# Last chunk of the MLP's second product: one seven-product run over all 1,024 output columns, in place of seven products for one half and a plain product for the other

## The chip, the cores and the metric

The kernel runs on one core of a Trainium2 chip. The metric is the device time of one execution in microseconds (us); lower is better. The engines are TensorE (PE in the profile; its weight loads are PEld), VectorE (DVE), ScalarE (ACT), GpSimd (POOL) and SyncE (SP, which here only issues DMAs). SBUF is the core's on-chip memory, PSUM the accumulators that TensorE writes; a PSUM bank holds 128 x 512 f32.

## What is computed

The reference is one decoder layer on 512 tokens of width 1,024. The change touches only its end:

```python
D_MODEL, SEQ, D_FF = 1024, 512, 4096
...
        x = x + merged @ w_out[l]
        h = rms_norm(x, norm_mlp[l])
        x = x + jnp.square(jax.nn.relu(h @ w_ff1[l])) @ w_ff2[l]
    return rms_norm(x, norm_final)
```

Everything is float32. TensorE multiplies in its faster fp32r form, so each operand is split into a high and a low part, and a product is three matmuls: high by high, high by low, low by high.

## The kernel before

**Chunks.** The hidden width of 4,096 is worked in four chunks of 1,024 (c = 0 to 3). In each chunk the first product makes 1,024 hidden columns for all 512 tokens, and the second product multiplies them by the chunk's 1,024 rows of `w_ff2` and adds the result into the residual `XX` (`x` in the profile), which stays in SBUF as four token tiles of 128 x 1,024.

**Seven products.** Most products are done in Strassen-Winograd form: both operands are cut into 2 x 2 blocks, and seven block products (named A11, S1, S3, A12, A22, S2, S4 after the weight block that each uses) take the place of eight. S1 to S4 are sums of the blocks A11 to A22 of the weight. The products share work: U is the A11 product (less the S2 product in the form before), and it is added into several quadrants of the result by the `fold` step.

**The second product, chunks 0 to 2** (class `Wide`, L1563): each of the seven products covers 512 output columns in two weight tiles (group g = 0, 1, each 128 x 1,024 floats = two k blocks of 512 columns), 12 matmuls of 512 columns for each tile.

**The second product, chunk 3** (`LAST`, L1872 to L1947): the left 512 output columns go by seven products of 256-column matmuls (class `Out`, L1517, 24 matmuls of 256 columns each, matmul line L1534). The right 512 columns are a plain product: four weight tiles of 256 rows (`f2310` to `f2313`), kept in the tiles R_64 and R_65 (`keep`), and for each of the four token tiles 24 matmuls of 512 columns (`last_half`, matmul line L505). The plain product of the token tiles 0 and 1 stands behind A11, S1 and A12; those of the token tiles 2 and 3 stand at the very end, the last one cut in two blocks of 256 columns. So the tokens of tiles 0 to 2 are normalized and sent out while TensorE still works for tile 3.

**A weight tile's way** (`group_steps`, L337): a DMA issued by SyncE brings it into one of five `raw` buffers; ScalarE copies the high part into one of three slots (wh, wh again, w3h; L357); VectorE subtracts to make the low part (wl, w3l; L360); TensorE reads both; the slot comes free when TensorE has done with it. The first use of a tile therefore waits for ScalarE, the second matmul for VectorE. Sums of weight blocks are made in two ways: in DRAM by DMAs (a copy, then an accumulating DMA issued by GpSimd, `make_sum` and `add_sum`), or in SBUF by VectorE from two raw buffers that lie there anyway (`SUMS`, L369, and L346 for the fourth). In chunk 3 before, all four sums of the left half come from DRAM.

**The order of the work** is written out by the program: `LAST_TURN` gives the turn of the products, `add_turn` the order of the loads, `ahead` (L479) starts the preparation of tiles up to three ahead, and side generators (`step_side`) interleave the steps on the results. Each engine then works its queue strictly in order.

**The hidden part** (class `Hidden`, L1764): its blocks get the same Winograd sums and high and low splits on VectorE and ScalarE (L1780, L1783, L1790, L1791, L1803 to L1817). In chunk 3 it also splits block 12 (into xT2), which only the plain product needs.

**The end**: for each token tile two square sums on ScalarE (L1502), one root and one reciprocal, two `scalar_tensor_tensor` on VectorE (L1514), and a DMA of 512 KB out. The last token tile is done in pieces on three engines (L1932 to L1947), with a 128 x 704 product on GpSimd (L1936).

Of the kernel before, what the change touches and what calls it, by code (L numbers as in the profile page):

```python
# [62 lines left out]
def trunk(ctx: ExitStack, tc: tile.TileContext, A, out):  # L63
# [124 lines left out]
    LAST_TURN = ("A11", "S1", "A12"), ("S3", "A22", "S2", "S4")  # L188

    def quarters(layer, c, g):  # L190

        if layer == 2 and c < LAST:
# [3 lines left out]
        w, r, o = ((w_f1, 0, 1024 * c + 512 * g), (w_f2, 1024 * c, 512 * g))[layer - 1]  # L196
        return {f"{i + 1}{j + 1}": w[r + 512 * j:r + 512 * j + 512, o + 256 * i:o + 256 * i + 256].rearrange(
            "(k p) c -> p k c", p=128) for i in range(2) for j in range(2)}

    def add_group(layer, c, g):  # L200
# [3 lines left out]
        final = layer == 2 and c == LAST  # L204
        for o in ("S1", "S3", "S2", "S4")[:4 if final else 4 - layer]:
# [7 lines left out]
        if final:  # L213
            jobs.append((of["S2"], of["S3"], q["22"]))
            jobs.append((of["S4"], of["S2"], q["12"]))
# [3 lines left out]
    SUMS = {"S2": "S4", "A12": "S4"}, {"S3": "S2", "A22": "S2", "S2": "S4"}  # L219

    def add_turn(layer, c, of, turn):
        for g, o in turn:
            key = f"{o}{layer}{c}{g}"
            to = SUMS[layer - 1].get(o) if "S4" not in of[g] else None
            if to:
                SUM_OF[key] = f"{to}{layer}{c}{g}"
            if layer == 2 and "S4" not in of[g] and o == "S4":
# [8 lines left out]
    for c in range(4):  # L236
# [98 lines left out]
    def rows_of(key):  # L335

        return 2 if key[-3] == "2" and int(key[-2]) < LAST else 4  # L337

    def group_steps(i):
# [15 lines left out]
        h, l = slot_of(i)  # L355
# [11 lines left out]
        else:  # L367
            yield
            DVE.tensor_tensor(t, t, held[to], op=ALU.add)  # L369
# [3 lines left out]
    kept = {}  # L373
# [1191 lines left out]
    class Wide(Out):  # L1565
# [40 lines left out]
        def fold(self):  # L1606
            for i, j in ((0, 1), (1, 0), (1, 1)):
                for f in range(2):
# [4 lines left out]
                    yield  # L1613

# [149 lines left out]
    class Hidden:  # L1764
# [4 lines left out]
        def __init__(self, last):  # L1769
            self.last = last  # L1770
# [4 lines left out]
        def of(self, b):  # L1775
            return XB["T2"] if b == "12" else YB[b]
# [22 lines left out]
        def sums(self, f):  # L1799
# [8 lines left out]
            if self.last:  # L1808
                yield from self.split("12", f, f12)
# [12 lines left out]
        def plain_of(self, k, t):  # L1822
            x = self.of(f"{k // 4 + 1}{t // 2 + 1}")
            return [y[:, k % 4, 128 * (t % 2):128 * (t % 2) + 128] for y in x]

    def in_turn(groups, turn):

        seen = {}
        for o in turn:
            n = seen.get(o, 0)  # L1830
            seen[o] = n + 1
            groups[n].pe(o)

    mode["pool"] = False
    for c in range(4):
        Y = Hidden(c == LAST)
# [35 lines left out]
    def last_half(w, t, cols=slice(0, 512), rows=range(4)):  # L1872

        prods = []
        for i in rows:
            for k in range(2):
                prods += split_products(*Y.plain_of(2 * i + k, t), w[i][0][:, k, cols], w[i][1][:, k, cols])
        return prods

    def folded():  # L1880
        yield from head.fold()
        for t in range(NT):
            square_sum(t, 0)
            yield
            if t < 2:
                finish(t)
                yield

    head = Out(LAST, 0, Y)
    keep([f"f2{LAST}1{i}" for i in range(4)], OT)  # L1890
    in_turn([head], LAST_TURN[0])
    w = []
    ps = [bank() for _ in range(2)]
    for i in range(4):
        w.append(use(f"f2{LAST}1{i}"))
        for t in range(2):
            mms(ps[t], last_half(w, t, rows=[i]), first=i == 0, last=i == 3)
            ahead()
            step_side()
    for t in range(2):  # L1900
        add_x(t, 1, ps[t])
        square_sum(t, 1)
    in_turn([head], LAST_TURN[1])
    gB = GBf[:, 0:D]
    nc.sync.dma_start(gB, bcast(A["norm_final"], D))
    while head.done != set(head.X):
        step_side()
    side.append(folded())
    END = 768
    xe = [x[:, 0, :] for x in XB["T3"]]  # L1910
    ACT.activation(xe[0], X1[3][:, END:], AF.Copy)
    DVE.tensor_tensor(xe[1], X1[3][:, END:], xe[0].bitcast(F32), op=ALU.subtract)
    for t in (2, 3):
        for c, n in (((0, 512),) if t == 2 else ((0, 256), (256, 256))):
            ps = bank()[:, 0:n]
            prods = last_half(w, t, slice(c, c + n))
# [49 lines left out]
```

## Time and profile before

| | |
|---|---|
| median of 3 runs | 787.26 us (786.37 to 789.39) |
| the profiled execution's own time | 786.53 us |
| its span, first to last instruction | 784.8 us |
| mean granted TensorE clock | 0.998 |
| busy: PE, DVE, ACT, POOL | 98%, 84%, 64%, 22% of the span |

The span is what the profile's clock covers; 1.73 us of the execution lie around it. In the rows of the timeline the columns are the start in us from the span's beginning, the duration in us, the engine, the line, the operation, out<-in by the program's names (without buffer numbers), the shape and the count; in square brackets stands the idle time before it and what ended it. A row with x2 merges two instructions. The last chunk's second product begins 735.3 us into the span and the last instruction of the chain that ends it is at 780 us; it takes 6% of the span.

### The profile page before, as it was taken

What the parts mean: (1) busy time and instruction counts of PE and PEld (TensorE: products, weight loads), DVE (VectorE), ACT (ScalarE), POOL (GpSimd) and SP (SyncE); (2) the same over time, 40 slices, a digit from 0 to 9 for tenths busy, and PEclk for the clock granted to TensorE, in tenths of its full rate; (3) what the DMA queues carried; (4) which work ended last, traced back from release to release, by engine and by line L of the source; (5) the groups of instructions that cost most, each with busy time, mean ns of one, the idle gap of its engine ahead of it and who ended that gap; (6) DMA issues with size and microseconds to landing.
All of it is one profiled execution on the core that took longest, in us unless ns stands there. A gap on an engine that the chain in (4) does not pass through costs nothing. (4 is left out here: it accounts for less than half of the span.)

```text
span 784.8 us, 13451 instructions
## 1 busy us (share of the span) xinstructions
PE 766.2 (98%) x4795; PEld 681.7 (87%) x4795; DVE 659.1 (84%) x1274; ACT 505.0 (64%) x977; POOL 175.2 (22%) x257
## 2 busy tenths in 40 slices
PE   7999999999999999999999999999999999999996
PEld 6889889888878888888889899879997999799996
DVE  6999868557989988998689689997899789998974
ACT  6668545337978888899545576944783478347833
POOL 4000000016847766553000120111110111010001
PEclk9999999999999999999999999999999999999999
DMA  9463732474565731011667998979998999897522
GB/s 306 129 165 98 198 95 91 116 209 122 77 162 112 165 66 41 28 55 50 170 212 210 286 239 241 299 172 312 306 268 221 309 282 286 213 273 219 189 78 108
DMA packets 118013, 140.80 MB, mean 179 GB/s; under 512 B 5477, under 2 KB 94729, under 8 KB 117770
## 3 DMA queue, kind: packets, MB, share of 16 engines
q1 hardware_dynamic: 98026, 116.64, 46.0%
q0 software_dynamic: 19632, 22.55, 19.2%
q8 instruction: 38, 0.62, 0.3%
q10 hardware_dynamic: 288, 0.75, 0.3%
q14 instruction: 29, 0.24, 0.1%
HBM read 135.20 MB, written 47.19 MB: 232 GB/s over the span
## 5 line engine op out<-in xcount | busy, mean ns | idle before, releaser
L505 PE MATMUL psF<-R,wh 128*128 128x512 f32 x448 | 144.3, 399 | 0.7 <-ACT scratch L876 0.7
L357 ACT ACTIVATE wh<-raw 128x1024 fp32r<-128x1024 f32 x70 | 73.8, 1058 | 70.0 <-PE psB L575 27.4
L319 POOL DMA_DIRECT2D S<-w_ff x40 | 45.1, 1128 | 307.3 <-DMA S<-w_ff 202.0
L360 DVE TENSOR_TENSOR wl<-raw,wh 128x1024 fp32r<-128x1024 f32 x70 | 85.3, 1221 | 18.5 <-ACT wh L357 18.3
L1323 POOL TENSOR_SCALAR P<-P,sm,GT 128x128 f32<-128x128 f32 (+3 forms) x128 | 85.2, 683 | 69.8 <-DVE sm L1320 44.4
L505 PEld LDWEIGHTS psF<-R,wh 128*128 128x128 f32 x448 | 80.5, 188 | 14.5 <-ACT scratch L876 0.9
L505 PE MATMUL psF<-R,wl 128*128 128x512 f32 x224 | 88.4, 394 | 1.3 <-DVE wl L464 1.3
L462 ACT ACTIVATE wh<-raw 128x512 fp32r<-128x512 f32 (+1 forms) x84 | 50.0, 620 | 55.9 <-PE psF L505 30.0
L1310 ACT ACTIVATE P<-P,sm 128x128 f32<-128x128 f32 (+3 forms) x128 | 71.2, 559 | 8.8 <-DVE sm L1300 6.0
L464 DVE TENSOR_TENSOR wl<-raw,wh 128x512 fp32r<-128x512 f32 (+1 forms) x82 | 56.6, 705 | 21.3 <-ACT wh L462 20.9
L1300 DVE CUSTOM_DVE_ANT_0 P<-psS,cst 128x128 f32<-128x128 f32 (+3 forms) x128 | 59.6, 483 | 4.6 <-PE psT L1340 2.5
L575 PE MATMUL psB<-R,wh 128*128 128x256 f32 x336 | 60.0, 279 | 0.0
L1356 DVE TENSOR_TENSOR PT<-psT,PT 128x512 fp32r<-128x512 f32 (+2 forms) x96 | 56.3, 592 | 3.5 <-ACT PT L1351 3.0
L357 ACT ACTIVATE w3h<-raw 128x1024 fp32r<-128x1024 f32 x35 | 37.0, 1058 | 31.2 <-PE psB L575 13.3
L1351 ACT ACTIVATE PT<-psT 128x512 fp32r<-128x512 f32 (+2 forms) x96 | 49.3, 522 | 12.0 <-PE psT L1340 10.9
L575 PEld LDWEIGHTS psB<-R,wh 128*128 128x128 f32 x336 | 51.4, 188 | 0.2
L505 PEld LDWEIGHTS psF<-R,wl 128*128 128x128 f32 x224 | 42.0, 188 | 10.4 <-DVE wl L464 1.7
L1340 PE MATMUL psT<-ident,P 128*128 128x128 f32 x320 | 50.1, 272 | 0.2 <-DVE PT L1356 0.2
L1374 PE MATMUL psO<-PT,VV 128*128 128x256 f32 x320 | 48.5, 286 | 0.0
L360 DVE TENSOR_TENSOR w3l<-raw,w3h 128x1024 fp32r<-128x1024 f32 x35 | 42.8, 1222 | 6.0 <-ACT w3h L357 5.9
L1340 PEld LDWEIGHTS psT<-ident,P 128*128 128x128 f32 x320 | 39.7, 140 | 8.9 <-issue 1.3
L575 PE MATMUL psB<-R,wl 128*128 128x256 f32 x168 | 46.9, 279 | 0.0
(487 smaller groups left out, 2210.1 us busy)
## 6 DMA issues: line engine op xcount, KB each, us to landing
raw<-w_ff SPq DMA_DIRECT2D x55, 512.0 KB, 6.8
S<-w_ff POOLq DMA_DIRECT2D x40, 512.0 KB, 8.4
raw<-S SPq DMA_DIRECT2D x40, 512.0 KB, 5.3
raw<-w_in SPq DMA_DIRECT2D x32, 512.0 KB, 4.0
S<-w_ff SPq DMA_DIRECT2D x30, 512.0 KB, 7.3
S<-S SPq DMA_DIRECT2D x10, 512.0 KB, 6.4
raw<-w_proj_nsa SPq DMA_DIRECT2D x8, 512.0 KB, 4.0
x<-x SPq DMA_DIRECT2D x7, 512.0 KB, 6.2
```

Of the source, the lines that this page charges most:

```text
L357: ACT.activation(h, t, AF.Copy)
L360: DVE.tensor_tensor(l, t, h.bitcast(F32), op=ALU.subtract)
L462: ACT.activation(h[:, sl], t[:, sl], AF.Copy)
L464: eng.tensor_tensor(l[:, sl], t[:, sl], h[:, sl].bitcast(F32), op=ALU.subtract)
L505: PE.matmul(ps, a, b, start=first and j == 0, stop=last and j == n - 1, skip_group_check=True)
L575: PE.matmul(out, w[u][:, k, 128 * f:128 * f + 128], moving[v][:, k, :], **kw)
L1300: DVE.tensor_tensor_reduce(out=P[:, o:o + n].rearrange("p (a c) -> p a c", c=128), in0=s, in1=m, scale=1.0, scalar=3e38, op0=ALU.add, op1= ...
L1310: last_exp[:] = [ACT.activation(c, c, AF.Exp, bias=sm[:, 0, e:e + 1], scale=-1.0, accum_out=sm[:, 1, e:e + 1])]
L1323: r = POOL.tensor_scalar(P[:, o:o + n], P[:, o:o + n], sm[:, 2, e:e + 1], GT[:, qb, c + e:c + e + 1], op0=ALU.mult, op1=ALU.mult)
L1340: PE.transpose(pt[:, 128 * j:128 * j + 128], P[:, 128 * j:128 * j + 128], ident)
L1351: ACT.activation(dH, src, AF.Copy)
L1356: return DVE.tensor_tensor(dL, src, dH.bitcast(F32), op=ALU.subtract)
```

## The change

For chunk 3 the new class `Whole` (a form of `Wide`) runs the seven products over all 1,024 columns, like the other chunks, in the turn A11, S1, S3, A22, S2, A12, S4. It differs from `Wide` in four ways.

1. No product accumulates on another one's PSUM bank, and U is the A11 product alone. VectorE adds each product straight from PSUM into every quadrant that needs it (`QUADS`, `take`: two for S1, two for S3, three for S2, one each for A22, A12, S4; two 128 x 512 additions for each quadrant).
2. GpSimd adds U into all four quadrants (`fold`: eight additions of 128 x 512). The additions for the last two quadrants stand behind the first two weight sums in GpSimd's queue (`pooled`).
3. The weight sums S2 = S3 + A22 and S4 = S2 + A12 are made in SBUF by GpSimd (four additions of 128 x 1,024), not in DRAM. S4's tiles go to the kept tiles R_64 and R_65.
4. S4, the last, works only on the right half of the tokens (token tiles 2 and 3, left 512 columns): 12 matmuls of 512 columns for tile 2, then two blocks of 12 matmuls of 256 columns for tile 3. Token tiles 0 and 1 are complete after A12.

The plain product, its four weight tiles, the split of block 12 and the function `folded` go. The end of the last token tile keeps its form with other column numbers.

```diff
-    LAST_TURN = ("A11", "S1", "A12"), ("S3", "A22", "S2", "S4")
+    LAST_TURN = ("A11", "S1", "S3", "A22", "S2", "A12", "S4")
...
-    SUMS = {"S2": "S4", "A12": "S4"}, {"S3": "S2", "A22": "S2", "S2": "S4"}
+    SUMS = [{"S2": "S4", "A12": "S4"}, {"S3": "S2", "A22": "S2", "S2": "S4"}]
+    SUMS.append(SUMS[0] | SUMS[1])
...
         else:
             yield
-            DVE.tensor_tensor(t, t, held[to], op=ALU.add)
+            last = key[-3:-1] == f"2{LAST}"
+            r = (POOL if last else DVE).tensor_tensor(t, t, held[to], op=ALU.add)
+            if last:
+                pooled.append(r)
             give_back(held[to])
             held[to] = t
...
+    class Whole(Wide):
+        AFTER = {}
+        QUADS = {"S1": ((1, 1), (0, 1)), "S3": ((1, 1), (1, 0)), "A22": ((1, 0),),
+                 "S2": ((1, 0), (1, 1), (0, 1)), "A12": ((0, 0),), "S4": ((0, 1),)}
+
+        def take(self, o, ps):
+            yield
+            if o == "A11":
+                for f in range(2):
+                    ACT.activation(self.U[:, f, :], ps[f], AF.Copy)
+                side.append(self.fold())
+            else:
+                for q in self.QUADS[o]:
+                    for f in range(2):
+                        self.add(DVE, q, f, ps[f], o == "S2")
+                        self.added(o, q, f)
+                    yield
+            self.done.add(o)
+
+        def add(self, eng, q, f, y, minus=False):
+            i, j = q
+            x = XX[:, 2 * j + f, 512 * i:512 * i + 512]
+            eng.tensor_tensor(x, x, y, op=ALU.add if bool(i) == minus else ALU.subtract)
...
+        def fold(self):
+            for q in ((0, 1), (1, 1), (1, 0), (0, 0)):
+                while q[1] == 0 and len(pooled) < 2:
+                    yield
+                for f in range(2):
+                    with behind(pooled[1]) if q[1] == 0 else nullcontext():
+                        self.add(POOL, q, f, self.U[:, f, :])
+                    yield
+                    yield
...
+    class Last(Whole):
+        def added(self, o, q, f):
+            t = 2 * q[1] + f
+            if o == "S2" and q[0] == 1:
+                square_sum(t, 1, 0)
+            elif o == "A12":
+                square_sum(t, 0, 1)
+                finish(t)
+
+    whole = Last(LAST, Y)
+    keep([f"S42{LAST}{g}" for g in range(2)], OT)
+    for o in LAST_TURN[:-1]:
+        whole.pe(o)
...
+    ps = bank()
+    for _ in pieces(ps, whole.ends(0)(slice(0, 512))):
+        step_side()
...
+    whole.add(DVE, (0, 1), 0, ps)
+    square_sum(2, 0, 1)
...
+    finish(2)
+    t, o, prods = 3, out_of(3), whole.ends(1)
+    for c in (END, 0):
+        ps = bank()[:, 0:256]
+        for _ in pieces(ps, ([(identR, x) for x in xe] if c == 0 else []) + prods(slice(c, c + 256))):
             step_side()
...
+        if c:
+            POOL.tensor_tensor(o[:, 320:D], X1[t][:, 320:D], gB[:, 320:D], op=ALU.mult)
```

How the queues stand is shown in two places. The first is GpSimd's queue from the last accumulating DMA to the end of the program. S_ tiles are sums in DRAM, raw_ the loaded weight tiles, x the residual, MA holds U and the output tiles, and GB the norm's weights. Before:

```order
L319 DMA S_131_108<-w_ff 512x1x256 [waits DMAHW6_49,DMASW0_49]
L319 DMA S_230_111<-w_ff 512x1x256 [waits DMAHW2_49,DMASW1_49]
L319 DMA S_230_112<-w_ff 512x1x256 [waits DMAHW7_49,DMASW2_49]
L1936 TENSOR_TENSOR MA<-x_4759,GB 128x704 [waits DMAHW5_49,DMAHW7_49,DVE_49,Activation_49]
L1943 TENSOR_SCALAR MA<-MA,sq 128x256 [waits DVE_49,Pool_49]
```

And in the changed kernel:

```order
L310 DMA S_231_112<-w_ff 256x1x512 [waits DMAHW6_49,DMASW2_49]
L1634 TENSOR_TENSOR x_4759<-x_4759,MA 128x512 [waits DVE_49,Activation_49]
L1634 TENSOR_TENSOR x_4759<-x_4759,MA 128x512 [waits DVE_49]
L1634 TENSOR_TENSOR x_4759<-x_4759,MA 128x512 [waits DMAHW5_49,Activation_49]
L1634 TENSOR_TENSOR x_4759<-x_4759,MA 128x512 [waits DVE_49]
L361 TENSOR_TENSOR raw_4766<-raw_4766,raw_5131 128x1024 [waits DMAHW2_49,DMAHW0_49,DVE_49]
L361 TENSOR_TENSOR raw_5170<-raw_5170,raw_5110 128x1024 [waits DMAHW3_49,DMAHW7_49,DMAHW1_49,DVE_49]
L1634 TENSOR_TENSOR x_4759<-x_4759,MA 128x512 x4
L361 TENSOR_TENSOR raw_5149<-raw_5149,raw_4766 128x1024 [waits DMAHW4_49,DVE_49,Pool_49]
L361 TENSOR_TENSOR raw_5131<-raw_5131,raw_5170 128x1024 [waits DMAHW6_49,DVE_49,Pool_49]
L1947 TENSOR_TENSOR MA<-x_4759,GB 128x704 [waits DMAHW5_49,DVE_49]
```

Twelve additions have come between the last DMA and the 128 x 704 product: eight of U and four of weight tiles, each with both inputs in SBUF.

The second place is VectorE's queue in the middle of the last chunk's second product. wl, w3l and R_65 are low parts of weight tiles, psB is a product in PSUM, and "waits Pool" is a wait for GpSimd. Before:

```order
L360 TENSOR_TENSOR wl_4995<-raw_5149,wh_4994 128x1024 [waits DMAHW4_49]
L360 TENSOR_TENSOR w3l<-raw_5131,w3h 128x1024 [waits DMAHW5_49]
L1498 TENSOR_TENSOR x_4759<-psB,x_4759 128x512 [waits PE_49] x2
L1554 TENSOR_TENSOR x_4759<-x_4759,psB 128x2x256 [waits DVE_49,PE_49]
L360 TENSOR_TENSOR wl_4958<-raw_5110,wh_4957 128x1024 [waits DMAHW6_49,DVE_49,Activation_49]
L1554 TENSOR_TENSOR x_4759<-x_4759,psB 128x2x256 [waits PE_49]
L1550 TENSOR_TENSOR MA<-MA,psB 128x512 [waits PE_49]
```

And in the changed kernel, from the low part of A22's second tile to S2's second tile and A12's first:

```order
L351 TENSOR_TENSOR wl_4995<-raw_5170,wh_4994 128x1024 [waits DMAHW3_49,Activation_49]
L351 TENSOR_TENSOR w3l<-raw_4766,w3h 128x1024 [waits Activation_49]
L1634 TENSOR_TENSOR x_4759<-x_4759,psB 128x512 [waits DVE_49]
L1634 TENSOR_TENSOR x_4759<-x_4759,psB 128x512 [waits DVE_49,PE_49]
L1634 TENSOR_TENSOR x_4759<-x_4759,psB 128x512 [waits Pool_49] x2
L351 TENSOR_TENSOR wl_4958<-raw_5170,wh_4957 128x1024 [waits Activation_49]
L351 TENSOR_TENSOR wl_4995<-raw_5149,wh_4994 128x1024 [waits DMAHW4_49,Activation_49]
```

The additions of S3 into a quadrant wait for GpSimd's addition of U to the same place, and the low parts of S2's second tile and of A12's first now stand behind them.

More of the change, by code (lines that the diff above doesn't have):

```diff
@@ L335, in rows_of @@
     def rows_of(key):
-        return 2 if key[-3] == "2" and int(key[-2]) < LAST else 4
+        return 2 if key[-3] == "2" else 4
     def group_steps(i):
@@ L1820, in sums @@
             yield from self.split("T4", f, f21)
[L1822 to L1832, printed above, removed]
     mode["pool"] = False
     for c in range(4):
-        Y = Hidden(c == LAST)
+        Y = Hidden()
         gs = [Group(f"1{c}{g}", XB.get, bank, (pair(GBf, 6 + g), pair(MAf, 6 + g), pair(MAf, 0), pair(MAf, 1)),
@@ L1889, in trunk @@
[L1889 to L1898, printed above, removed]
-            step_side()
[L1900 to L1904, printed above, removed]
@@ new lines, in trunk @@
+    ps = bank()
+    for _ in pieces(ps, whole.ends(0)(slice(0, 512))):
+        step_side()
+    until(lambda: whole.done >= set(LAST_TURN[:-1]))
+    drain_side()
+    whole.add(DVE, (0, 1), 0, ps)
+    square_sum(2, 0, 1)
+    END = 256
+    xe = [x[:, 0, :] for x in XB["T3"]]
+    ACT.activation(xe[0], X1[3][:, 0:END], AF.Copy)
+    DVE.tensor_tensor(xe[1], X1[3][:, 0:END], xe[0].bitcast(F32), op=ALU.subtract)
+    finish(2)
[3 more added lines that the diff above has]
+        for _ in pieces(ps, ([(identR, x) for x in xe] if c == 0 else []) + prods(slice(c, c + 256))):
+            step_side()
+        x = ps
+        if c:
+            x = X1[t][:, c:c + 256]
+            DVE.tensor_tensor(x, ps, x, op=ALU.add)
+        junk = p4.tile([128, 512], F32, tag="junk", bufs=1, name="junk")
+        ACT.activation(junk[:, 0:256], x, AF.Square, accum_out=sq[:, t, 1:2])
+        if c:
+            POOL.tensor_tensor(o[:, 320:D], X1[t][:, 320:D], gB[:, 320:D], op=ALU.mult)
+            DVE.tensor_scalar(sq[:, t, 2:3], sq[:, t, 1:2], 1.0 / D, sq[:, t, 2:3], op0=ALU.mult, op1=ALU.add)
@@ new lines, in trunk @@
+    ACT.activation(sq[:, t, 3:4], sq[:, t, 1:2], AF.Sqrt, bias=sq[:, t, 2:3], scale=1.0 / D)
+    DVE.reciprocal(sq[:, t, 4:5], sq[:, t, 3:4])
+    r = sq[:, t, 4:5]
+    ACT.activation(o[:, 576:D], o[:, 576:D], AF.Copy, scale=r)
+    POOL.tensor_scalar(o[:, 320:576], o[:, 320:576], r, 1.0, op0=ALU.mult, op1=ALU.mult)
+    for y, cs in ((ps, slice(0, END)), (X1[t][:, END:320], slice(END, 320))):
+        DVE.scalar_tensor_tensor(o[:, cs], y, r, gB[:, cs], op0=ALU.mult, op1=ALU.mult)
+    for cs, q in ((slice(576, D), ACT), (slice(0, 576), nc.sync)):
+        q.dma_start(out_d[128 * t:, cs], o[:, cs])
```

119 lines of the change are left out of this document (34 added, 85 removed).

## The prediction

> **What bounds the kernel now.** I read the page first, then the chain of work that ended last, then who kept TensorE waiting in the last stage, and then VectorE's and GpSimd's queues there in order of time. The engines over the whole span:
>
> ```profile
> span 784.8 us, 13451 instructions
> ...
> PE 766.2 (98%) x4795; PEld 681.7 (87%) x4795; DVE 659.1 (84%) x1274; ACT 505.0 (64%) x977; POOL 175.2 (22%) x257
> ```
>
> TensorE is never free for long. The chain of work that ended last, in order of time (start, us, what), shows it for the end of the kernel (the last three rows are the last square sum, root and reciprocal):
>
> ```profile
> 668.98 26.61 PE psB L1584 x116
> ...
> 744.66 10.91 PE psB L505 x48
> 755.57 11.65 PE psB L1534 x96
> 767.22 11.46 PE psB L505 x74
> 778.68 0.02 issue
> 778.70 0.48 ACT junk L1934 x2
> ...
> 779.21 0.30 ACT sq L1939
> ...
> 779.54 0.17 DVE sq L1940
> ```
>
> From 744.66 to 778.68 us the chain is TensorE alone; only then come 1.0 us of small steps to the reciprocal (779.71), and 784.8 - 779.71 = 5.1 us of scaling and output DMA. The waits of TensorE from 700 us on, longest first, and the first matmul of the last chunk's second product:
>
> ```profile
> PE psB L575 <- DVE MA L596: 0.4, 1, 0.4
> PE psB L1534 <- ACT MA L1548: 0.3, 1, 0.3
> ```
> ```profile
> 735.30 0.29 PE L1534 MATMUL psB<-wh,y11H 128*128 128x256 f32 x1
> ```
>
> So in this stage TensorE waits for 0.3 us in 43. The other engines have slack, but less than the page's average says (columns: the stretch, its length, then busy us of PE, PEld, DVE, ACT, POOL):
>
> ```profile
> 740.00:760.00 20.00, 19.70 (x121) 17.51 (x120) 18.07 (x28) 12.68 (x22) 0.00 (x0) 1.00 0.41 137
> 760.00:785.00 25.00, 18.66 (x135) 17.44 (x133) 11.62 (x26) 6.37 (x19) 2.18 (x2) 0.94 0.22 85
> ```
>
> VectorE is nearly full up to 760 us and half empty behind it; GpSimd does nothing at all until 760.
>
> **TensorE's own time.** Before, the stage has 168 matmuls of 256 columns by seven products (0.121 us each, 11.65/96), and the plain product's 72 of 512 columns and 50 of 256 (with two that add the residual). 48 of 512 take 10.91 us, 0.227 each, so of the last 11.46 us 24 x 0.227 = 5.5 are for 512 columns and 6.0 for the 50 short ones. Sum: 20.4 + 16.4 + 6.0 = 42.8 us. After, there are 156 of 512 columns at 0.229 us (26.61/116, the same form in chunk 2) and 26 short ones at 0.12: 35.8 + 3.1 = 38.9 us. The wait for L1548 goes too, since A12 no longer accumulates on A11's bank. Term: **-3.9 us**, -4.2 with the wait, if TensorE stays the bound. Each weight tile is now used for 12 x 0.229 = 2.75 us.
>
> **VectorE's and GpSimd's new work.** How long VectorE's steps take, from their starts in a stretch where it never pauses: 0.60 us for 128 x 512, also from PSUM, and 1.14 for a low part of 128 x 1,024 (752.20 - 751.06). A `scalar_tensor_tensor` takes 0.67 (776.18 - 774.85 for two). One-column steps start 0.05 to 0.1 apart.
>
> ```profile
> 749.26 0.68 DVE L1554 TENSOR_TENSOR x<-x,psB 128x512 f32<-128x512 f32 x1
> 749.86 0.69 DVE L1783 TENSOR_TENSOR yT3L<-GB,yT3H 128x512 fp32r<-128x512 f32 x1
> 750.46 0.69 DVE L1783 TENSOR_TENSOR yT2L<-MA,yT2H 128x512 fp32r<-128x512 f32 x1
> 751.06 1.22 DVE L360 TENSOR_TENSOR wl<-raw,wh 128x1024 fp32r<-128x1024 f32 x1
> 752.20 0.69 DVE L1554 TENSOR_TENSOR x<-x,psB 128x512 f32<-128x512 f32 x1
> ```
> ```profile
> 774.85 1.41 DVE L1514 SCALAR_TENSOR_TENSOR MA<-x,sq,GB 128x512 f32<-128x512 f32 x2
> 776.18 0.42 DVE L1932 TENSOR_TENSOR x<-psB,x 128x256 f32<-128x256 f32 x1
> ```
> ```profile
> 767.86 0.16 DVE L1511 RECIPROCAL sq<-sq 128x1 f32<-128x1 f32 x1
> 767.93 0.14 DVE L1504 TENSOR_SCALAR sq<-sq 128x1 f32<-128x1 f32 x1
> 767.98 0.69 DVE L1560 TENSOR_TENSOR x<-x,MA 128x512 f32<-128x512 f32 x1
> ```
>
> GpSimd's additions, by the two groups of the page's kind that come nearest (last figures before the bar: busy us, mean ns of one):
>
> ```profile
> L464 POOL TENSOR_TENSOR wl<-raw,wh 128x512 fp32r<-128x512 f32 x4 | 5.1, 1286 | 2.5 <-ACT wh L462 2.5
> L1936 POOL TENSOR_TENSOR MA<-x,GB 128x704 f32<-128x704 f32 x1 | 1.7, 1711 | 63.1 <-DVE x L1932 63.1
> ```
>
> An addition of U is the first form: 1.29 us, eight make 10.3. A 128 x 1,024 sum isn't in the trace: by the slope between the two rows, 425 ns for 192 columns, it is 1.286 + 512 x 2.21 ns = 2.42 us; by plain doubling it is 2.57. I take 2.42; four make 9.7.
>
> **Do the two engines get in each other's way?** This decides the case. Three places in the trace, GpSimd and VectorE side by side:
>
> ```profile
> 297.70 0.77 POOL L1323 TENSOR_SCALAR P<-P,sm,GT 128x512 f32<-128x512 f32 x1 [2.04 <-DVE sm L1320]
> ```
> ```profile
> 297.85 1.15 DVE L464 TENSOR_TENSOR wl<-raw,wh 128x512 fp32r<-128x512 f32 x1
> ```
> ```profile
> 266.76 0.40 POOL L1239 TENSOR_SCALAR PC<-cw 128x256 fp32r<-128x256 f32 x1
> 266.80 0.90 DVE L464 TENSOR_TENSOR wl<-raw,wh 128x512 fp32r<-128x512 f32 x1
> ...
> 267.24 1.06 POOL L1240 TENSOR_TENSOR PC<-cw,PC 128x256 fp32r<-128x256 f32 x1
> ```
> ```profile
> 286.99 0.73 POOL L815 TENSOR_TENSOR rs<-rs,cst 128x256 f32<-128x256 f32 x1
> ```
> ```profile
> L815 POOL TENSOR_TENSOR rs<-rs,cst x10: 730/738/1158, 190.3 to 316.5; 128x256 f32<-128x256 f32 x10
> ```
> ```profile
> 287.36 0.67 DVE L1356 TENSOR_TENSOR PT<-psT,PT 128x512 fp32r<-128x512 f32 x1
> ```
> ```profile
> 293.00 0.74 POOL L1240 TENSOR_TENSOR PC<-cw,PC 128x256 fp32r<-128x256 f32 x1
> ```
>
> (The row with three figures is GpSimd's L815 over the whole span: shortest, median and longest in ns.) VectorE's low part of 128 x 512 takes 0.69 us alone, as in the row at 749.86. At 297.85 it takes 1.15 and ends at 299.00, which is 0.53 us after GpSimd's end (298.47): it waited until GpSimd had finished and then ran its elements. At 266.80 it ends at 267.70, 0.54 after GpSimd's end at 267.16; and now GpSimd's next step, begun at 267.24, takes 1.06 us where it takes 0.74 at 293.00: it ends 0.60 after VectorE's end. So they take turns, whoever was first holding the other up, when both read two inputs from SBUF. At 287.36 VectorE reads one input from PSUM, and both run beside each other at their usual times, 0.73 and 0.67 us. The Trainium skill has this as a rule (SBUF — State Buffer, section Who interferes with whom): a VectorE instruction with two SBUF inputs and a GpSimd instruction that reads SBUF share one read interface, and the second fully blocks; one SBUF input doesn't contend. These rows agree with it, and the rule speaks against this change.
>
> **The sum under turns.** Count from the stage's first matmul, 735.3, to the low part of S4's second tile, the last that TensorE needs. In that stretch VectorE has 13 low parts of weight tiles (13 x 1.14 = 14.8 us) and 12 steps of the hidden part (12 x 0.60 = 7.2), all with two SBUF inputs; GpSimd has 10.3 + 9.7 = 20.0. Only one of them can run at a time: 42.0 us, so that the last low part is ready at 777.3 at the earliest, where without turns it is needed (12 tiles and a half by then) at 735.3 + 12.5 x 2.75 = 769.7. VectorE's PSUM additions (12 in this stretch) can run beside GpSimd. The queues' order shows where TensorE is held: the additions of U (5.2 us for the first four) fall among the low parts of S1's and S3's tiles, and S2's second tile stands on VectorE behind S3's additions, which wait for GpSimd's seventh step. What TensorE has left waits behind it.
>
> What is behind the last low part on VectorE, in order: 7 PSUM additions left (4 of S2, 2 of A12, 1 of S4; 4.2 us), the 256-wide addition and xT3L (0.4 each), nine one-column steps (about 0.1 each, 0.9), six `scalar_tensor_tensor` (4.0): 9.9 us. GpSimd's 704-column product falls into the last of them and holds one up (1.6 of its 1.71), and the last root comes in between (0.3 + 0.17). Together 12.0 us to the last reciprocal, at 789.3. Before, token tiles 0 to 2 were finished while TensorE still had 5.5 us for tile 3, and VectorE was idle at the end; now S4's matmuls are through before VectorE is, by some 6 us. The end costs 5.1 us as before: 794.4. Against the span, 784.8: **+9.6 us**. The profiled execution took 786.53 us, 0.73 under the median of the runs shown; 786.53 + 9.6 = 796.1, I say **796.0**.
>
> **What costs nothing or little.** The right half's eight half-tile low parts, the split of block 12 and two DRAM sums go; the sum above counts what is left, so nothing is credited twice. The rows on ScalarE's copies, on the weight loads (KB, median us from issue to landing) and on the output DMAs:
>
> ```profile
> L357 ACT ACTIVATE wh<-raw 128x1024 fp32r<-128x1024 f32 x70 | 73.8, 1058 | 70.0 <-PE psB L575 27.4
> ```
> ```profile
> raw<-w_ff SPq DMA_DIRECT2D x55, 512.0 KB, 6.8
> ```
> ```profile
> out_dram<-MA SPq DMA_DIRECT2D x3, 512.0 KB, 2.6
> ```
>
> ScalarE's 14 copies are 14.8 us beside 38.9; the cover is that ScalarE was busy for only 12.7 of 20 us in this stretch, and without it each copy would cost its 1.06. SyncE has one load less; A12's second tile now waits for the raw buffer that GpSimd's first sum frees, under turns at 735.3 + 6 low parts (6.8) + 7.2 + 4 additions of U (5.2) + the sum (2.4) = 756.9; it lands 6.8 us later, at 763.7, and its low part isn't due before 769 (777.3 less two sums, two low parts and itself): nothing, unless a load takes over 11 us. Token tile 2's 512 KB now leave about 1 us before the last pieces, not 4; if these wait for its landing, 2.6 - 1: 0 to +1.6, I take 0.
>
> **The range of this case.** GpSimd's steps without their start-up, hidden behind a wait (about 0.14 each, 1.06 less 0.60 and the like): -1.7; by plain doubling of the wide sum: +0.6. The stretch begins earlier by 0.6 if VectorE, freed from the block 12 split, is ahead when the stage begins, or later by 1. The 704 product gets out of the way: -1.6. Gaps in which neither holds the interface, because a sum waits for the low part in front of it: 0 to +2. Not all at once: 792.5 to 799.5.
>
> **The rivals.**
> *No turns here* (not slower). The additions overlap freely, and low parts keep 1.2 us while GpSimd adds. Then TensorE runs its 38.9 us from 735.3 with under 1 us of stalls, to 775. A12's second tile gets its slot when nine tiles are used up, at 760.1; its copy and low part are through at 763.4, GpSimd's last sum at 765.9, and S4's second low part at 768.2. Behind it VectorE's queue is 9.9 us, with 1.2 us of waits for square sums and roots: 779.3, 0.4 before today: **786.1**. So even then VectorE's tail takes 3.5 of the 3.9 us. Against it stand the rows at 266.80 and 297.85; for it, only that those are other tiles.
> *Part of the turns.* GpSimd holds the interface for only half of each step: 22.0 + 10.0 us of turns, and 12 PSUM additions (7.2) half hidden, about 36 in place of 42.0; half of the 704 product's 1.6 goes too: 6.8 less, **789.3**. Against it, VectorE at 297.85 waited for GpSimd's very end.
> *TensorE stays the bound* (faster): all of -4.2, **782.3**. Against it: behind S2's last matmul VectorE has the 9.9 us, two more additions and S4's two low parts, 13.4 in all, and TensorE only 38.9 - 27.5 = 11.4.
>
> **How the numbers follow.** A measurement of this kernel can tell about 0.5% (3.9 us, so to 790.5) from no change. Forecast, turns in full: 0.78. Part of the turns: 0.08. No turns: 0.11. TensorE's bound: 0.03. So faster 0.03, same 0.19, slower 0.78. The range reaches from 788.5 (a little under part of the turns) to 800.0 and leaves out the two cases without turns.
>
> **What would show it.** Right: low parts (L351) that take 1.5 to 3.5 us whenever GpSimd's L361 or L1634 runs, and GpSimd steps above 1.29 and 2.42; TensorE waiting for VectorE's wl at S3 and S2, some 8 us in all between 745 and 783; the last reciprocal 5 to 7 us after the last matmul, with `scalar_tensor_tensor` in between. Wrong: low parts at 1.2 us beside GpSimd (then 786), waits of TensorE for a DMA or for ScalarE, or a last matmul after 785 us.

## The result, and the profile after

The changed kernel takes 797.22 us (median of 4 runs, 796.82 to 797.40) against 786.82 us before (4 runs, 785.22 to 789.39): ratio 1.0128, 95% interval 1.0100 to 1.0156. It is slower by 10.4 us; 796.0 us was forecast, 1.2 less than measured. The profiled execution took 797.40 us, 1.8 more than its span, and the span is 10.8 us longer than before (795.6 - 784.8), where +9.6 was forecast. The page of the changed kernel, with the chain that ended last, by engine, in the last row:

```profile
span 795.6 us, 13261 instructions
...
PE 766.2 (96%) x4687; PEld 676.2 (85%) x4687; DVE 669.6 (84%) x1278; ACT 506.5 (64%) x975; POOL 207.1 (26%) x269
...
DVE 2%; POOL 1%; issue 1%; ACT 0%; ACTq 0%; DVEq 0%; POOLq 0%
```

TensorE is busy for as long as before and has gone from the chain that ended last. The end of that chain in order of time (start, us, what):

```profile
761.70 2.51 POOL x L1634 x2
...
766.47 2.30 DVE wl L351
...
772.52 3.41 POOL raw L361
...
778.56 1.79 DVE x L1634 x3
...
783.04 1.42 DVE MA L1509 x2
...
786.83 2.73 DVE MA L1509 x2
...
790.62 0.17 DVE sq L1950
```

GpSimd and VectorE hand it to each other until the last weight sum, at 775.9; from 778.5 on it is VectorE's queue, where the kernel before had TensorE until 778.7. Who kept TensorE waiting from 700 us on:

```profile
PE psB L1579 <- DVE wl L351: 4.5, 2, 3.5
PE psB L499 <- DVE xT3L L1933: 0.8, 1, 0.8
PE psB L499 <- DVE R L351: 0.8, 1, 0.8
PE psB L499 <- ACT R L348: 0.5, 1, 0.5
PE psB L499 <- ACT xT3H L1932: 0.3, 1, 0.3
```

All five lie in the last stage: 6.9 us there, in place of 0.3. The same two stretches as were shown for the kernel before, with the same columns (PE, PEld, DVE, ACT, POOL busy; then clock, DMA share, GB/s):

```profile
740.00:760.00 20.00, 16.46 (x71) 12.97 (x71) 15.72 (x21) 8.87 (x13) 18.59 (x6) 0.99 0.31 101
760.00:785.00 25.00, 21.09 (x92) 16.14 (x90) 19.53 (x29) 10.31 (x20) 13.48 (x7) 0.94 0.01 3
```

GpSimd, idle until 760 before, now stands as busy for 18.59 of the first 20 us and 13.48 of the next 25. But busy here includes being held, as its own queue shows (start, us, line, what; in brackets the idle time in front):

```profile
740.25 14.56 POOL L1634 TENSOR_TENSOR x<-x,MA 128x512 f32<-128x512 f32 x4 [31.86 <-ACT MA L1621]
754.76 2.36 POOL L361 TENSOR_TENSOR raw<-raw,raw 128x1024 f32<-128x1024 f32 x1
758.28 3.42 POOL L361 TENSOR_TENSOR raw<-raw,raw 128x1024 f32<-128x1024 f32 x1 [1.16 <-DVE wl L351]
761.67 6.02 POOL L1634 TENSOR_TENSOR x<-x,MA 128x512 f32<-128x512 f32 x4
```

The same view cut to the stretch from 740 to 741 us shows the first of these additions by itself:

```profile
740.25 10.81 POOL L1634 TENSOR_TENSOR x<-x,MA 128x512 f32<-128x512 f32 x1 [31.86 <-ACT MA L1621]
```

An addition that should take 1.29 us takes 10.81. VectorE's queue beside it and after it:

```profile
747.56 1.22 DVE L351 TENSOR_TENSOR w3l<-raw,w3h 128x1024 fp32r<-128x1024 f32 x1
748.70 1.22 DVE L351 TENSOR_TENSOR wl<-raw,wh 128x1024 fp32r<-128x1024 f32 x1
752.35 0.69 DVE L1634 TENSOR_TENSOR x<-x,psB 128x512 f32<-128x512 f32 x1 [2.43 <-POOL x L1634]
754.84 1.88 DVE L1634 TENSOR_TENSOR x<-x,psB 128x512 f32<-128x512 f32 x3 [1.81 <-POOL x L1634]
756.64 1.56 DVE L351 TENSOR_TENSOR wl<-raw,wh 128x1024 fp32r<-128x1024 f32 x1
758.25 1.23 DVE L351 TENSOR_TENSOR w3l<-raw,w3h 128x1024 fp32r<-128x1024 f32 x1
...
764.84 3.93 DVE L351 TENSOR_TENSOR wl<-raw,wh 128x1024 fp32r<-128x1024 f32 x2
...
769.89 2.49 DVE L351 TENSOR_TENSOR w3l<-raw,w3h 128x1024 fp32r<-128x1024 f32 x1
...
777.04 1.23 DVE L351 TENSOR_TENSOR R<-raw,R 128x1024 fp32r<-128x1024 f32 x1 [2.19 <-ACT R L348]
...
786.75 2.82 DVE L1509 SCALAR_TENSOR_TENSOR MA<-x,sq,GB 128x512 f32<-128x512 f32 x2
```

Until 749.92 VectorE runs one step with two SBUF inputs after another, each at its usual 0.69 or 1.22 us. GpSimd's first addition ends at 751.06, 1.14 us after the last of them. By itself it takes 1.29, so it can have done little or nothing before (an estimate from these rows). Then VectorE itself has to wait, first for the second of the four additions and then for the fourth (2.43 and 1.81 us idle). From 754.76 on it goes to and fro: the low parts at 756.64, 764.84 and 769.89 are held (two take 3.93 where 2.36 is usual, as in e4's row at 757.77 below), while the one at 758.25 runs at 1.23 and GpSimd's sum beside it takes 3.42 in place of 2.36.

### The profile page after: what moved, and what is told of

It reads as the page before. It is cut to its first block, busy times and chain, and to the rows that moved or that the text cites. A ratio compares the mean times of both kernels' runs of the same rounds, so it can differ in the third digit from the quotient of the medians.

```text
span 795.6 us, 13261 instructions
## 1 busy us (share of the span) xinstructions
PE 766.2 (96%) x4687; PEld 676.2 (85%) x4687; DVE 669.6 (84%) x1278; ACT 506.5 (64%) x975; POOL 207.1 (26%) x269
## 5 line engine op out<-in xcount | busy, mean ns | idle before, releaser
L348 ACT ACTIVATE wh<-raw 128x1024 fp32r<-128x1024 f32 x73 | 76.9, 1057 | 76.4 <-PE psB L569 27.2
L351 DVE TENSOR_TENSOR wl<-raw,wh 128x1024 fp32r<-128x1024 f32 x73 | 90.8, 1247 | 18.3 <-ACT wh L348 18.0
L456 ACT ACTIVATE wh<-raw 128x512 fp32r<-128x512 f32 (+1 forms) x84 | 49.9, 618 | 56.2 <-PE psF L499 29.9
L348 ACT ACTIVATE w3h<-raw 128x1024 fp32r<-128x1024 f32 x37 | 39.1, 1056 | 41.8 <-PE psB L569 13.3
L1350 DVE TENSOR_TENSOR PT<-psT,PT 128x512 fp32r<-128x512 f32 (+2 forms) x96 | 56.2, 592 | 3.4 <-ACT PT L1345 3.0
L351 DVE TENSOR_TENSOR w3l<-raw,w3h 128x1024 fp32r<-128x1024 f32 x37 | 46.5, 1256 | 5.9 <-ACT w3h L348 5.8
L499 PEld LDWEIGHTS psF<-R,wl 128*128 128x128 f32 x224 | 42.1, 188 | 10.3 <-DVE wl L458 1.8
L1334 PEld LDWEIGHTS psT<-ident,P 128*128 128x128 f32 x320 | 39.7, 140 | 8.8 <-issue 1.2
```

Source lines behind the costliest of these rows:

```text
L348: ACT.activation(h, t, AF.Copy)
L351: DVE.tensor_tensor(l, t, h.bitcast(F32), op=ALU.subtract)
L456: ACT.activation(h[:, sl], t[:, sl], AF.Copy)
L499: PE.matmul(ps, a, b, start=first and j == 0, stop=last and j == n - 1, skip_group_check=True)
L1334: PE.transpose(pt[:, 128 * j:128 * j + 128], P[:, 128 * j:128 * j + 128], ident)
L1350: return DVE.tensor_tensor(dL, src, dH.bitcast(F32), op=ALU.subtract)
```

## Experiments

**Theories.** *Turns*: VectorE's steps with two SBUF inputs and GpSimd's additions exclude each other, and the lost time is what GpSimd holds. *Slow partner* (rival): VectorE's steps wait for what GpSimd computes because GpSimd is slow, not because they share anything. *VectorE's own queue* (rival): the form of the products gives VectorE too much to do, with or without GpSimd. Ratios are to the kernel before, run beside each of them. The start of the last chunk's second product differs by up to 2.2 us between the profiled executions of before, the change and e1 to e8 (733.52 to 735.70), so the length of this last stage, from its first matmul to the end of the span, is given too. In the changed kernel it starts with this row of TensorE:

```profile
735.03 0.39 PE L1579 MATMUL psB<-wh,y11H 128*128 128x512 f32 x1
```

So the stage takes 795.6 - 735.03 = 60.6 us, and 784.8 - 735.30 = 49.5 before. The others, worked out in the same way:

| version | stage, us | median, us | ratio (95%) |
|---|---|---|---|
| the change | 60.6 | 797.2 | 1.0128 (1.0100 to 1.0156) |
| e1 sums on VectorE | 58.9 | 794.3 | 1.0096 (1.0077 to 1.0115) |
| e2 U on VectorE | 57.8 | 793.9 | 1.0090 (1.0072 to 1.0108) |
| e3 both on VectorE | 56.2 | 792.6 | 1.0075 (1.0057 to 1.0093) |
| e4 GpSimd only writes | 51.2 | 787.3 | 1.0013 (1.0001 to 1.0026) |
| e5 U's sums unread | 58.7 | 794.6 | 1.0109 (1.0091 to 1.0127) |
| e6 scaling on ScalarE | 58.6 | 795.2 | 1.0111 (1.0089 to 1.0133) |
| e7 DRAM sums, U on VectorE | 53.8 | 790.6 | 1.0051 (1.0033 to 1.0068) |
| e8 e7, tail off VectorE | 54.8 | 789.4 | 1.0043 (1.0028 to 1.0058) |
| e9 e7, sums early | 52.2 | 815.0 | 1.0363 (1.0344 to 1.0381) |
| e10 e8, sums early | 50.6 | 811.4 | 1.0320 (1.0302 to 1.0338) |
| e11 before, sums early | 49.3 | 799.9 | 1.0166 (1.0127 to 1.0204) |
| e12 e8, sums in time | 54.3 | 798.5 | 1.0165 (1.0143 to 1.0186) |

Each stage length comes from one profiled execution. The intervals of e1, e2, e5 and e6 overlap that of the change, so what is said below of gains of 2 to 3 us rests on the medians and the stage lengths together and is less certain than e3 and e4, whose intervals lie apart from it.

**e1: the weight sums on VectorE.**

```diff
-            r = (POOL if last else DVE).tensor_tensor(t, t, held[to], op=ALU.add)
+            r = DVE.tensor_tensor(t, t, held[to], op=ALU.add)
```

> The changed kernel with the four weight sums on VectorE; GpSimd keeps the eight additions of U. Three theories. Turns (VectorE's steps with two SBUF inputs and GpSimd's additions exclude each other): 9.7 us of GpSimd leave the stretch that can't overlap and 4 x 1.14 = 4.6 us of VectorE enter it, so 797.2 - 5.1 = about 792 us. Slow partner (VectorE and ScalarE only wait in their queues for a slow GpSimd, without any exclusion): VectorE's and ScalarE's waits for the sums (about 5 us in the trace of the changed kernel) go and 4.6 us come, about 797. VectorE's own queue (the added additions and the squeezed end are the loss, GpSimd has no part in it): 4.6 us more, about 802.

**e2: the additions of U on VectorE.**

```diff
-                        self.add(POOL, q, f, self.U[:, f, :])
+                        self.add(DVE, q, f, self.U[:, f, :])
```

> The changed kernel with the eight additions of U on VectorE; GpSimd keeps the four weight sums. Turns: 10.3 us of GpSimd go from the stretch, 8 x 0.60 = 4.8 come, about 791.7 us. Slow partner: VectorE's waits for U (7.1 us in the trace of the changed kernel) go, 4.8 come, about 795. VectorE's own queue: about 802.

**e3: both.**

> The changed kernel with both the weight sums and U's additions on VectorE, so that GpSimd does nothing in the stage but the 704-column product at the end. VectorE's steps up to the last low part add up: 22.0 + 4.8 + 4.6 two-input steps and 7.2 us of PSUM additions, 38.6 from 735.2, so the last low part at 773.8 in place of 778.2. Turns: 4.4 us and the waits at the end less, about 792 us: VectorE doing all of it is faster than VectorE with GpSimd's help. Slow partner: 9.3 us of waits go, 9.4 come, about 797. VectorE's own queue: 9.4 us more, about 806.

e1 and e2 took 794.3 and 793.9, gains of 2.9 and 3.4 us where turns had forecast 5 and more. That is far from VectorE's own queue (802), but e1 lies between turns (792) and the slow partner (797), and e2 lies nearer to the slow partner's 795 than to turns' 791.7: these two don't decide between them. e3 does: it took 792.6, as turns had forecast (792), where the slow partner had 797 and VectorE's own queue 806. VectorE doing all of the work is faster than VectorE with GpSimd's help. Why e1 fell short stands in its own waits of VectorE and then of TensorE:

```profile
DVE x L1634 <- POOL x L1634: 6.7, 2, 4.2
```
```profile
PE psB L1579 <- ACT w3h L348: 5.8, 1, 5.8
```

U's first addition starves as in the changed kernel, VectorE's queue stops for it and everything behind stops too, the low parts and sums on which the next slot hangs. In e2 the PSUM additions, which ran beside GpSimd's U, have lost part of that cover; this is argued only. In e3 VectorE never pauses, and its steps can be added up: 13 low parts and 4 sums at 1.14 and 12 + 8 + 13 steps at 0.60 (of the hidden part, of U, and with a PSUM input) make 39.2 us. Its last low part and its last reciprocal:

```profile
771.73 1.22 DVE L351 TENSOR_TENSOR R<-raw,R 128x1024 fp32r<-128x1024 f32 x1
...
784.76 0.16 DVE L1950 RECIPROCAL sq<-sq 128x1 f32<-128x1 f32 x1 [0.93 <-ACT sq L1949]
```

With 1.14 us for itself, the low part is through 39.35 us after the first matmul (733.52). So the rival has a part of the truth: VectorE's queue alone, full, is a bound of its own, 6.3 us above the kernel before (792.6 - 786.3).

**e4: GpSimd as busy, but reading nothing.**

```diff
-            r = (POOL if last else DVE).tensor_tensor(t, t, held[to], op=ALU.add)
+            if last:
+                for _ in range(4):
+                    r = POOL.memset(t, 0.0)
+            else:
+                DVE.tensor_tensor(t, t, held[to], op=ALU.add)
...
-                        self.add(POOL, q, f, self.U[:, f, :])
+                        i, j = q
+                        for _ in range(3):
+                            POOL.memset(XX[:, 2 * j + f, 512 * i:512 * i + 512], 0.0)
```

> Each addition of GpSimd in the stage becomes three or four memsets of the same place, which write and read nothing (so U and the weight sums are left out of the result); every engine still waits for GpSimd at the same places, and GpSimd is busy for about as long (about 1.2 us in place of 1.29, 2.4 to 2.7 in place of 2.42). Turns: nothing is shared any more, VectorE's low parts run at 1.14 us beside GpSimd, and the time falls to that of the prediction's rival without turns, 786 to 788 us. Slow partner: the waits stay, 796 to 797. VectorE's own queue: 797.

It took 787.3 us. GpSimd's queue in the last stage:

```profile
749.36 7.93 POOL L363 MEMSET raw<- 128x1024 f32 x8 [38.01 <-DVE wl L351]
757.23 5.67 POOL L1651 MEMSET x<- 128x512 f32 x12
762.85 7.45 POOL L363 MEMSET raw<- 128x1024 f32 x8
```

That is 21.0 us of work, where the additions make 20.0 by themselves, and ScalarE still waits 3.8 us for one of the memsets. The 12 memsets that stand for U's first four additions ran ahead of the stage, nine at 698 and three at 709, as they need no U. VectorE's low parts beside these rows all take their usual time:

```profile
757.77 2.36 DVE L351 TENSOR_TENSOR wl<-raw,wh 128x1024 fp32r<-128x1024 f32 x2 [2.06 <-ACT wh L348]
...
762.44 1.22 DVE L351 TENSOR_TENSOR w3l<-raw,w3h 128x1024 fp32r<-128x1024 f32 x1
```

So a busy GpSimd costs little by itself, and so does the work that VectorE has left: what GpSimd reads is what costs, up to 60.6 - 51.2 = 9.4 us of stage. Up to, because in e4 VectorE doesn't wait for U at all, where it waits 7.1 us in the change; e5 takes these waits away and leaves the reads, and it saves only 1.9 us of stage. (The Trainium skill says this in SBUF — State Buffer, section Who interferes with whom: the contention is with a GpSimd instruction that reads SBUF, not with one that only writes it. These rows agree.) Without turns nothing is left of the gain, as the prediction's rival *no turns* had it (786.1). The last matmul of e4:

```profile
776.23 0.28 PE L503 MATMUL psB<-R,y22L 128*128 128x256 f32 x1
```

It ends 42.1 us after the first (734.42), 1.3 earlier than before (778.66 - 735.30 = 43.4); but 9.1 us follow it, not 6.1, because VectorE's end comes behind it.

**e5: additions of U that nobody reads.**

```diff
-                        self.add(POOL, q, f, self.U[:, f, :])
+                        POOL.tensor_tensor(XB["T2"][0][:, 0:2, :], self.U[:, f, :].rearrange("p (k t) -> p k t", k=2),
+                                           self.U[:, f, :].rearrange("p (k t) -> p k t", k=2), op=ALU.add)
```

> The changed kernel, but GpSimd's eight additions read U twice and write to a tile that nothing reads, so U is left out of the result: the same GpSimd work with two SBUF inputs, and no VectorE step waits for it. In the changed kernel VectorE waits 7.1 us for GpSimd's additions to x. Turns (what is lost is the time in which only one of the two can run): the exclusive work is the same 42 us, and VectorE's waits only move to steps that are held: 795 to 797.5. Waits (what is lost is VectorE's idle time behind late GpSimd results): 4 to 7 us less, 790 to 793.

794.6 us, 58.7 of stage: 1.9 less than the change, between the two forecasts and nearer to turns. GpSimd's first additions are starved as before, though nothing hangs on them:

```profile
738.93 14.78 POOL L1645 TENSOR_TENSOR xT2H<-MA 128x512 fp32r<-128x512 f32 x4 [30.35 <-ACT MA L1621]
```

VectorE's 7.1 us of waits for GpSimd were thus mostly time in which GpSimd's work had to be done anyway; the rest, 1.9 us by one execution of each, is the price of the order.

**e6: the scaling of the token tiles 0 to 2 on ScalarE.**

```diff
-        normed(t, o)
+        ACT.activation(sq[:, t, 3:4], sq[:, t, 1:2], AF.Sqrt, bias=sq[:, t, 2:3], scale=1.0 / D)
+        DVE.reciprocal(sq[:, t, 4:5], sq[:, t, 3:4])
+        ACT.activation(o, X1[t], AF.Copy, scale=sq[:, t, 4:5])
```

> The changed kernel, but the token tiles 0 to 2 are scaled by ScalarE (one activation of 128 x 1,024 each), which leaves out the final norm's weights for them: six scalar_tensor_tensor of 0.67 us go from VectorE. If VectorE's queue behind the last low part sets the end, as the prediction's 12.0 us of queue say, this gives 4.0 us and up to 1.4 more that one of them lost beside GpSimd's 704-column product: 792 to 793.5. If the end is set by TensorE's late last matmul, 797 as before.

795.2 us, 2.0 less: half of what VectorE's queue alone would have given, and between the two forecasts, so that both missed. The last low part and the last reciprocal:

```profile
777.72 1.23 DVE L351 TENSOR_TENSOR R<-raw,R 128x1024 fp32r<-128x1024 f32 x1 [2.19 <-ACT R L348]
...
789.33 0.16 DVE L1952 RECIPROCAL sq<-sq 128x1 f32<-128x1 f32 x1 [1.51 <-ACT sq L1951]
```

From the one's end to the other's it is 10.6 us, where the change has 12.6, and now VectorE waits for ScalarE, whose square sums and three scalings (1.05 each) fill it. So VectorE's queue does set the changed kernel's end. ScalarE's takes over after 2 us, with three scalings in it that the change doesn't give it; how close it stands without them isn't shown.

**e7 and e8: can the form pay at all?** Here S2 and S4 come from DRAM sums, as before the change, and VectorE adds U. In e8 GpSimd also weighs the token tiles 0 to 2 in halves and ScalarE scales them.

```diff
+        final = layer == 2 and c == LAST
-        for o in ("S1", "S3", "S2")[:4 - layer]:
+        for o in ("S1", "S3", "S2", "S4")[:4 if final else 4 - layer]:
...
+        if final:
+            jobs.append((of["S2"], of["S3"], q["22"]))
+            jobs.append((of["S4"], of["S2"], q["12"]))
...
-    SUMS.append(SUMS[0] | SUMS[1])
+    SUMS.append({})
...
-                        self.add(POOL, q, f, self.U[:, f, :])
+                        self.add(DVE, q, f, self.U[:, f, :])
```
```diff
+    def weigh(t, h):
+        c = slice(512 * h, 512 * h + 512)
+        POOL.tensor_tensor(out_of(t)[:, c], X1[t][:, c], gB[:, c], op=ALU.mult)
...
+        weigh(t, 0)
...
+        ACT.activation(o, o, AF.Copy, scale=sq[:, t, 4:5])
```

> The changed kernel, but S2 and S4 come from DRAM sums, as in the form before, and VectorE adds U: GpSimd has no two-input step until the 704-column product, and VectorE has four steps of 1.14 us less than in the version without GpSimd's additions. Turns with a full VectorE queue: 26.8 us of two-input steps and 7.2 of PSUM additions put the last low part at 769.3, and 12.0 us of queue and 5.1 of end behind it make 786.4, so 788 by the clock of an execution; from the version without GpSimd's additions, 792.6 - 4.6 = 788.0. If something else holds that version (loads, slots, ScalarE): 791 to 793. TensorE's bound: 782 to 784.

> The version with DRAM sums and U on VectorE, and besides this the output of the token tiles 0 to 2 is made without VectorE: GpSimd multiplies x by the norm's weights in halves of 128 x 512 (six steps) as they are complete, ScalarE scales by the reciprocal. If VectorE's queue is what keeps 4 us of TensorE's saving: 4 us less than the other version, 784 to 785, faster than the kernel before by 0.2 to 0.4%. If GpSimd's six steps hold VectorE's last low parts and scalar_tensor_tensor steps up as much as they relieve it: 787 to 789. The form before would be equalled only, if the last pieces bind: 786 to 787.

790.6 and 789.4 us. In both, S1's second weight tile was loaded before A22 had been added to it in DRAM, so that this tile holds A21 alone, and its load doesn't wait for the rest of that sum; the work is the same otherwise. e7 lies between its first two forecasts (788, and 791 to 793); e8 lies 0.4 us above the highest of its three (787 to 789). In both a load stands in the chain that ended last. In e7's:

```profile
757.01 7.39 DMA raw<-S
```

S4's first tile (the expectations of e9 and e10 call it the second) arrives 7.4 us after its buffer is free, 8.7 in e8, beside the last DRAM sums, and TensorE waits 1.6 and 3.6 us for its high part.

**e9, e10 and e11: the DRAM sums begun earlier**, in e7, e8 and the kernel before.

```diff
-        return i < MLP0 + 6 or i % 3 == 0
+        return i < MLP0 + 6 or i % 3 == 0 or i % 6 == 1
```

> The version with DRAM sums and U on VectorE, with the DRAM sums of the last two chunks begun earlier (one more of six loads starts one), so that no sum's DMA is left for the last stage; in the run before this one two such copies and two accumulations ran there beside 98% busy DMA engines, and S4's second tile came 7.4 us after its buffer was free, at 764.4. Turns with a full VectorE queue: that load takes 3 to 5 us, the last low part is ready 1 to 3 us earlier: 787 to 789. If the loads are held by something else: 790 to 791.

> The same with the output of the token tiles 0 to 2 made by GpSimd's multiplications in halves and ScalarE's scaling. In the run before it TensorE waited 3.6 us for ScalarE's copy of S4's second tile, whose load came late. If that load is in time: 785 to 786.5, level with the kernel before; if ScalarE's queue at the end takes VectorE's place: 787.5 to 789.

> The kernel before with the same earlier DRAM sums and nothing else, a control for the two others. If the earlier sums only move DMA work to where it is hidden: within 0.2% of the kernel before. If they delay the loads of chunks 0 to 2: 1 to 3 us slower, and the two others are to be read against this one.

All three are far slower, the control too: 13.9 us more than the kernel before it (799.86 against 785.92), and its last stage, 49.3 us, has no part in that. The forecasts for e9 and e10 missed by 22 us and more, and that for the control, at most 3 us, by 11: the earlier sums aren't hidden in chunks 0 to 2. The control has 13.9 of e9's 29.1 us and of e10's 25.5; the rest isn't explained by a run. A stretch of e11 there, to be read by its first figure behind the length (TensorE's busy time) and its last three (clock, DMA share, GB/s; the share adds up the time that packets took and can pass 1):

```profile
500.00:600.00 100.00, 94.42 (x571) 83.31 (x569) 83.35 (x102) 60.51 (x83) 14.63 (x13) 0.98 1.08 295
```

and the same stretch of the kernel before:

```profile
500.00:600.00 100.00, 98.11 (x590) 86.11 (x590) 89.74 (x110) 61.79 (x83) 10.09 (x9) 1.00 0.94 262
```

The DMA engines were 94% busy already; with the share at 1.08 TensorE is busy for 3.7 us less. That the full DMA engines are the whole reason is argued only: from 600 to 700 us e11 loses another 3.5 us of TensorE, at a share of 0.77. The last stage of e10 is still worth reading by itself, since TensorE waits for no load and no GpSimd step in it. Its first matmul:

```profile
758.92 0.39 PE L1583 MATMUL psB<-wh,y11H 128*128 128x512 f32 x1
```

and GpSimd's six multiplications with two SBUF inputs, while all of VectorE's steps of 128 x 512 read PSUM:

```profile
793.28 7.75 POOL L1906 TENSOR_TENSOR MA<-x,GB 128x512 f32<-128x512 f32 x6 [111.42 <-DVE x L1638]
```

They take 7.75 / 6 = 1.29 us each, unhindered. The stage takes 809.5 - 758.92 = 50.6 us. So with the turns gone, the tail off VectorE and the loads in time, the form of the change is still 1.1 us longer than the 49.5 of the kernel before. VectorE's queue is full there: it is busy for all of the first 30 us of this stage.

**e12: the extra sums only from the middle of chunk 2 on.**

```diff
-        return i < MLP0 + 6 or i % 3 == 0
+        return i < MLP0 + 6 or i % 3 == 0 or i > MLP0 + 66 and i % 6 == 1
```

> The version without VectorE's scaling and without two-input steps of GpSimd, with the extra DRAM sums begun only from the middle of chunk 2, so that they are done when the last stage begins. With the sums begun early its last stage took 50.6 us from the first matmul to the end of the span (809.5 - 758.92), against 49.5 in the kernel before (784.8 - 735.30) and 60.6 in the changed one; what it lost was lost ahead of that stage. If the later pace hides the sums: the stage begins at 735 and the execution takes 787 to 788, no gain over the kernel before. If the DMA engines are full in chunks 2 and 3 all the same: 790 to 800. Faster than the kernel before, by under 0.3%, only if the stage also loses its 1.6 us of waits.

798.5 us, inside the second forecast, though not by its reason: the DMA share is 0.96 from 600 to 700 us, as before (0.97), and 0.73 from 700 to 780. The chain that ended last goes from 701.40 to 741.21 through DRAM sums one after another, the first for 15.00 us, and then a load. The stage begins 7 us late and is 54.3 us long:

```profile
742.42 0.50 PE L1583 MATMUL psB<-wh,y11H 128*128 128x512 f32 x1 [0.71 <-ACT wh L352]
```

No version tried beats the kernel before.

## Why the prediction was right, point by point

- **Turns decide the case: right.** e4 and e5 together show it. Without GpSimd's reads the same occupancy costs 0.13% (0.01 to 0.26%) over the kernel before; with them 1.28%. The rival *no turns* was right about the time of its own case, 787.3 against 786.1, and about VectorE's end eating what TensorE saves; but TensorE saved less than it said, 42.1 us to the last matmul where it had 39.7 (775 - 735.3).
- **What excludes what: read too narrowly.** The prediction says that the engines take turns "when both read two inputs from SBUF". But GpSimd's steps at 297.70 and 266.76 read one tensor each, with columns of factors at most, and VectorE's two-input step waited for them all the same. On GpSimd's side, reading one tensor from SBUF was enough. The sum doesn't change, since all of GpSimd's additions here have two inputs.
- **42.0 us to the last low part: right in size.** It ends at 777.04 + 1.14 = 778.2, 43.1 us after the first matmul, where the forecast had 42.0 and 777.3. The bound of 0 to 2 us for gaps in which neither engine holds the interface was needed: from 775.92, the end of the last sum, to 777.04 ScalarE makes its copy, 1.1 us. The range's start-up of 0.14 us is 0.74 less 0.60, by the rows at 293.00 and 267.24, and not "1.06 less 0.60".
- **The 128 x 1,024 sum at 2.42 us: right**; 2.36 unhindered (754.76). GpSimd's held steps were above this, as expected.
- **Where TensorE waits: half wrong.** The step that failed is "the additions of U (5.2 us for the first four) fall among the low parts of S1's and S3's tiles". They didn't: VectorE's run drew GpSimd's first addition out to 10.81 us, S1's and S3's tiles came at their usual times, and TensorE had no wait at S3. The debt was paid later, at A22's second tile (3.54 us, at 758.26) and S2's second (0.98). The sum hardly minds, since it only counts what excludes each other, in whatever order. TensorE waited for 6.9 us, not 8. So the sign "low parts (L351) that take 1.5 to 3.5 us whenever GpSimd's L361 or L1634 runs" is seen from 756 us on only; until 750 the low parts take 1.22 beside L1634. And 0.8 of the 6.9 us are waits for ScalarE, which the prediction had named as a sign against itself.
- **12.0 us of VectorE behind the last low part: right**, 12.6, with the 704-column product in it as said: the two steps at 786.75 take 2.82 us in place of 1.41.
- **5.1 us of end: right**, 795.6 - 790.79 = 4.8. Together 43.1 + 12.6 + 4.8 = 60.6 us (rounded) against 59.1.
- **The last reciprocal 5 to 7 us after the last matmul: right.** That one is here:

```profile
784.19 0.28 PE L499 MATMUL psB<-R,y22L 128*128 128x256 f32 x1
```

  It ends at 784.5, 6.2 us ahead of the reciprocal.

What stays open: how much of 10.4 us a different order of GpSimd's queue would have saved. e5 puts the price of this order at 1.9 us of stage, but an order in which U's first additions are through ahead of VectorE's run wasn't tried.

## What to carry to other kernels

Work with two SBUF inputs that went from a full VectorE to an idle GpSimd wasn't offloaded here at all: with all of it on VectorE (e3) the kernel is 4.6 us faster. Count VectorE's two-input steps and GpSimd's steps that read SBUF as one queue. What ran freely were GpSimd steps that only write, beside VectorE's two-input steps (e4), and VectorE steps that read PSUM, beside GpSimd's two-input steps (e10). A saving in matmuls is worth what the next engine's queue leaves of it, so add up that queue from the stage's first matmul to its last step before crediting TensorE's part. And a sum that goes to DRAM isn't free where the DMA engines are 94% busy: begun earlier, such sums cost the kernel before 13.9 us (e11).

## What the runs showed of the hardware that was not expected

- The exclusion wasn't a fair alternation. A VectorE queue of two-input steps without a pause drew a GpSimd addition of 1.29 us out to 10.81 (10.82 in e1 and 10.57 in e5, by the longest of their groups); it ended only after that run of VectorE's had ended. VectorE's steps lost nothing by it.
- A long stall of TensorE costs more than its length. After the 3.54 us at 758.26 the granted clock fell to 0.71 in the stretch from 760 to 765 us, and matmuls of 512 columns started 0.43 us apart, where 0.229 is usual:

```profile
758.26 0.50 PE L1579 MATMUL psB<-wl,yT4H 128*128 128x512 f32 x1 [3.54 <-DVE wl L351]
...
760.82 0.63 PE L1579 MATMUL psB<-wh,yT4H 128*128 128x512 f32 x1
761.25 0.63 PE L1579 MATMUL psB<-wl,yT4H 128*128 128x512 f32 x1
```

  It lasts from 759.5 to 762.5, seven matmuls, 1.4 us. The same follows the waits of 5.8 us in e1 (0.50 from 760 to 765) and 2.5 us in e3 (0.66 from 765 to 770), but not those of 1.6 us in e7 and 1.5 us in e2, after which the clock stays at 1.00. That it cost nothing here, as VectorE and GpSimd were the bound, is argued only.
